# RWKV preparation: head sums and low-rank products from parts, value transposes behind the gram, TensorE in a written order

## The chip, the cores and the metric

One NeuronCore of a Trainium2 chip runs the whole kernel. A core has a matrix engine (TensorE, PE in the profile), a vector engine (VectorE, DVE), an engine for functions of one argument (ScalarE, ACT), a general engine (GpSimd, POOL) and a queue engine for transfers (SyncE, SP). Each works through its own queue of instructions in order; between engines they wait for one another by semaphores. The metric is the device time of one execution in microseconds.

## The reference

One decoder block on 512 tokens of width 1024: RMSNorm, one wide input projection, two mixers (sparse attention and RWKV-7), a gated merge, an output projection, and a gated feed-forward layer. The change concerns the first half of the RWKV mixer, up to the vectors that its recurrence works on:

```python
r, k, v, xw, xa, xg = jnp.split(xl, RWKV_SPLITS, axis=-1)
w = -jax.nn.softplus(-(w0 + jnp.tanh(xw) @ w2)) - 0.5
decay = jnp.exp(-jnp.exp(w.astype(jnp.float32)))
a = jax.nn.sigmoid(a0 + xa @ a2)
...
kk = k * k_k.reshape(H, N).astype(jnp.float32)
kk = kk / jnp.maximum(jnp.sqrt(jnp.sum(kk * kk, axis=-1, keepdims=True)), 1e-12)
k = k * (1.0 + (a - 1.0) * k_a.reshape(H, N).astype(jnp.float32))
...
y = y + jnp.sum(r * k * r_k, axis=-1, keepdims=True) * v
```

There are eight heads of size 64. `xw @ w2` and `xa @ a2` are the two low-rank products (rank 64 each). The two sums over a head's 64 channels, of `kk * kk` and of `r * k * r_k`, are the head sums.

## The kernel before

Dense products are formed from parts: a float32 weight tile `raw` is copied by ScalarE into `whi` (float32r, line 129), VectorE subtracts to get `wlo` (line 339), and a 128-column product takes 24 matmuls of 128x512: 16 with `whi` (against the high and low parts `hh`, `hl` of the normalized input) and 8 with `wlo`. `whi` and `wlo` have two buffers each, so a new tile's parts can be written only when the tile before last has been read. `wnext` loads a tile and splits the next one.

The RWKV preparation works on heads in four pairs, p = 0 to 3, channels on partitions and the 512 tokens along the row. For each pair:

- `front(p)`: dense product for k; the low-rank pair `zw`, `za` from `wa` and `xw` (64 rows each, in the two halves of the array); token shift into `kx` (lines 129, 478); then the decay: `cl` (tanh, scale), a running sum in chunks (`cum`, line 540), and `ep`, `pi` (its exponentials).
- `norms(p)`: squares `kk` on ScalarE, their head sum by a product with a block matrix `ones`, and from it `rn` (maximum on VectorE, line 136; logarithm and exponential on ScalarE).
- `receptance(p)`: dense product for r, shifted into `rx`. `values_of(p)`: dense product for v, into `vx`.
- `values_tok(p)`: four transposes of `vx` on TensorE (line 578), copied into `UV`.
- `vectors(p)`: VectorE's chain from `rx`, `kx`, `rn`, `ep`, `pi` to `AR`, `bh` and `tv`, then the head sum of `tv` (the bonus sum) and `BO`, its product with `vx`.
- `gram(p)`: transposes of `bh` (line 609), copied into `BKT`, and products of `bh` with `AR`, masked into `AB`.

A loop over p runs `front` and `norms` of the next pair, then `values_tok`, `vectors`, `receptance` of the next, `gram`, and `values_of` of the next; one pass of it is called a visit here. Its rows below carry the numbers of the next pair for k, r and v, and those of this pair for the rest. `front(0)`, `norms(0)`, `receptance(0)` and `values_of(0)` stand ahead of the loop.

In this stage no order is written by hand: a scheduler places the instructions of every engine by its own estimates and by which buffers are free, and the outcome is a fixed queue per engine. PSUM has four banks `mm` and two each of `a` and `b`, used in rotation. A visit takes five of the `a` banks in turn (`zw`, squares, bonus sum, transposes, gram), so the gram's first products land in the bank of the bonus sum, which must have been read by `BO`.

Of the kernel before, what the change touches and what calls it, by code (L numbers as in the profile page):

```python
# [12 lines left out]
F32 = mybir.dt.float32  # L13
F32R = mybir.dt.float32r
I32 = mybir.dt.int32
AF = mybir.ActivationFunctionType
ALU = mybir.AluOpType
# [4 lines left out]
S = 512  # L22
D = 1024
NT = S // 128
KT = D // 128
DH = 64
H = 8
NH2 = H // 2
# [55 lines left out]
def hybrid_block(ctx: ExitStack, tc: tile.TileContext, A: dict, out: bass.AP):  # L84
    nc = tc.nc
# [30 lines left out]
    def pa():  # L116
        return bank("a", 2)
# [4 lines left out]
    def mm(o, l, r, start, stop):  # L122
        te.matmul(o, lhsT=l, rhs=r, start=start, stop=stop)  # L123
# [4 lines left out]
    def act(o, i, f=AF.Copy, **kw):  # L128
        sc.activation(o, i, f, **kw)  # L129

    def tt(o, a, b, op):
        return v.tensor_tensor(o, a, b, op=op)  # L132
# [12 lines left out]
    ident, mask, ones, cmask = kc[:, 0:128], kc[:, 128:256], kc[:, 256:384], kc[:, 384:416]  # L145
# [20 lines left out]
    for name in ("rwkv_mu", "rwkv_w0", "rwkv_a0", "rwkv_k_k", "rwkv_k_a", "rwkv_r_k", "rwkv_ln_g", "rwkv_ln_b"):  # L166
        r0, n = ROWS[name]
# [6 lines left out]
    def col(name, i=0):  # L174
        r0, n = ROWS[name]
        return prm[:, r0 + i:r0 + i + 1]
# [41 lines left out]
    hh = hp.tile([128, KT, S], F32R, name="hh", tag="hh")  # L218
# [154 lines left out]
    with tc.manual_schedule(engines={getattr(mybir.EngineType, e) for e in ("PE", "Activation", "DVE", "Pool")}):  # L373
# [10 lines left out]
        for t in range(NT):  # L384
            r = ssx[:, t:t + 1]
# [42 lines left out]
    def run(g):  # L428
        while True:
            try:  # L430
                next(g)
            except StopIteration as e:
                return e.value

    def dense_fm_g(xh, xl, kt=KT):
        hi, lo = wnext(kt, 128)
        p = mmb()
        for k in range(kt):
            mm(p, hi[:, k], xh[:, k], k == 0, False)
            mm(p, hi[:, k], xl[:, k], False, False)  # L440
            if 4 * k == 3 * kt - 4:
                yield
        for k in range(kt):
            mm(p, lo[:, k], xh[:, k], False, k == kt - 1)
        return p

    def dense_fm(xh, xl, kt=KT):
        return run(dense_fm_g(xh, xl, kt))
# [18 lines left out]
    scanm = tp.tile([128, NCH, C], F32, name="scanm")  # L467
    v.memset(scanm, 1.0)
    v.memset(scanm[:, :, 0:1], 0.0)
    wa = tp.tile([128, 512], F32, name="wa")  # L470
    nc.gpsimd.dma_start(wa[0:64], A["rwkv_w2"][0])
    nc.gpsimd.dma_start(wa[64:128], A["rwkv_a2"][0])
    nc.sync.dma_start(g2, A["rwkv_g2"][0])

    def shift_mix(p, m, dst):
        mu = col("rwkv_mu", m)
        act(dst, p, AF.Copy, scale=omm[:, m:m + 1])
        return v.scalar_tensor_tensor(dst[:, 1:], p[:, :-1], mu, dst[:, 1:], op0=ALU.mult, op1=ALU.add)

    def t2(name, bufs=1):  # L480
        return tp.tile([128, S], F32, name=name, tag=name, bufs=bufs)

    xw = t2("xw")
    shift_mix(p0, 12, xw)
    act(xw[0:64], xw[0:64], AF.Tanh)
    shift_mix(dense_fm(hh, hl), 13, sg)

    act(sg, sg, AF.Tanh, scale=0.5)
# [37 lines left out]
    def front(p):  # L526
        cs = slice(128 * p, 128 * p + 128)
        kx = t2("kx", 2)
        pk = dense_fm(hh, hl)
        zw, za = pa(), pb()  # L530
        mm(zw, wa[0:64, cs], xw[0:64], True, True)
        mm(za, wa[64:128, cs], xw[64:128], True, True)
        shift_mix(pk, 4 + p, kx)
        cl = t2("cl")
        act(cl, zw, AF.Tanh, scale=0.5, bias=w0h[:, p:p + 1])
        aa = t2("aa", 2)
        act(aa, za, AF.Tanh, scale=0.5, bias=a0h[:, p:p + 1])
        ts(cl, cl, -0.5 * DECAY, -0.5 * DECAY)
        cum = t2("cum")
        v.tensor_tensor_scan(out=cum, data0=scanm.rearrange("p c t -> p (c t)"), data1=cl, initial=0.0,  # L540
                             op0=ALU.mult, op1=ALU.add)
        ep = tp.tile([128, NCH, C + 1], F32, name="ep", tag="ep", bufs=2)
        v.memset(ep[:, :, 0:1], 1.0)
        act(ep[:, :, 1:], chunks(cum), AF.Exp)
        pi = t2("pi", 2)
        act(pi, cum, AF.Exp, scale=-1.0)
        v.tensor_copy(PC[:, p, :, None], ep[:, :, C:C + 1])
        L[p] = dict(kx=kx, aa=aa, ep=ep, pi=pi)

    def norms(p):  # L550
        kx = L[p]["kx"]
        kk = t2("kk", 2)
        act(kk, kx, AF.Square, scale=col("rwkv_k_k", p))
        ss = pa()
        mm(ss, ones, kk, True, True)
        rn = t2("rn", 2)
        ts(rn, ss, 1e-24, None, op0=ALU.max)
        act(rn, rn, AF.Ln)
        act(rn, rn, AF.Exp, scale=-0.5)
        L[p].update(kk=kk, rn=rn)  # L560

    def receptance(p):
        rx = t2("rx", 2)
        shift_mix(dense_fm(hh, hl), p, rx)
        L[p]["rx"] = rx

    def values_of(p):
        vx = t2("vx")
        mixed = shift_mix(dense_fm(hh, hl), 8 + p, vx)
        if p == NH2 - 1:  # L570
            behind.append(mixed)
        L[p]["vx"] = vx

    def values_tok(p):
        vx = L[p]["vx"]
        pt = pb()
        for i in range(4):
            te.transpose(pt[:, 128 * i:128 * i + 128], vx[:, 128 * i:128 * i + 128], ident)  # L578
        for r in range(2):
            for cc in range(2):  # L580
                act(UV[64 - 64 * r:128 - 64 * r, cc::2, p, r, :],
                    pt[64 * cc:64 * cc + 64].rearrange("p (c r d) -> p c r d", r=2, d=DH)[:, :, r, :])

    def vectors(p):
        kx, aa, ep, pi, kk, rn, rx, vx = (L[p][k] for k in ("kx", "aa", "ep", "pi", "kk", "rn", "rx", "vx"))
        stt(AR[:, p, :, 1, :], chunks(rx), 1.0, ep[:, :, 1:], ALU.mult, ALU.mult)
        stt(kk, kx, col("rwkv_k_k", p), rn, ALU.mult, ALU.mult)
        stt(AR[:, p, :, 0, :], chunks(kk), -1.0, ep[:, :, 0:C], ALU.mult, ALU.mult)
        stt(kk, aa, 1.0, kk, ALU.add, ALU.mult)
        bh = tp.tile([128, NCH, 3, C], F32, name="bh", tag="bh")  # L590
        stt(bh[:, :, 0, :], chunks(kk), 0.5, chunks(pi), ALU.mult, ALU.mult)
        v.tensor_copy(bh[64:128, :, 2, :], bh[64:128, :, 0, :])
        ts(aa, aa, kah[:, p:p + 1], oma[:, p:p + 1])
        stt(kx, kx, 1.0, aa, ALU.mult, ALU.mult)
        stt(bh[:, :, 1, :], chunks(kx), 1.0, chunks(pi), ALU.mult, ALU.mult)
        tv = t2("tv")
        stt(tv, rx, col("rwkv_r_k", p), kx, ALU.mult, ALU.mult)
        L[p]["bh"] = bh
        bs = pa()
        mm(bs, ones, tv, True, True)  # L600
        tt(BO[:, p], bs, vx, ALU.mult)

    def gram(p):
        bh = L[p]["bh"]
# [18 lines left out]


    front(0)
    norms(0)
    receptance(0)
    values_of(0)
    late_params()
    for p in range(NH2):  # L630
        if p + 1 < NH2:
            front(p + 1)
            norms(p + 1)
        values_tok(p)
        vectors(p)
        if p + 1 < NH2:
            receptance(p + 1)
        gram(p)
        if p + 1 < NH2:
            values_of(p + 1)  # L640
        if p + 2 == NH2:
            kcp = dense_fm(hh, hl)
    dbg("AR", AR)
    dbg("BO", BO)
    close(tp_cm)
# [1432 lines left out]
```

## Time and profile before

| what | value |
|---|---|
| median of 3 runs | 797.16 us (796.86 to 798.89) |
| profiled execution, its own time | 796.68 us |
| its span, first to last instruction | 794.9 us |
| granted TensorE clock | 1.000 |
| TensorE busy | 787.9 us (99%) |
| VectorE / ScalarE / GpSimd busy | 640.0 / 468.1 / 121.2 us |
| start of the preparation's pairs to the last gram | 29.7 to 120.4 us |

In the rows that follow, the first number is the start in microseconds from the first instruction, the second the duration; then come engine, line, operation, the tile written and the tiles read, and in brackets the idle time ahead of it with what ended it. Line 123 is the helper for matmuls and line 129 that for ScalarE, so the tiles say which step it is. The profile prints float32r operands of matmuls as f32. A float32 product of 512 columns shows as two rows, or as x2.

### The profile page before, as it was taken

Reading aid. Unit: us, or ns where it says so; the run is one execution under the profiler, and the core shown is the slowest. Engines: PE = TensorE matmul, PEld = TensorE weight load, DVE = VectorE, ACT = ScalarE, POOL = GpSimd, SP = SyncE. Lnnn points to the kernel's source line nnn. Section 1 sums busy time; section 2 is a strip of 40 time slices with the busy share of each in tenths; the row PEclk is TensorE's granted clock in tenths of the full one; section 3 lists DMA queues with packets and bytes.
Section 4 is the critical chain, followed back from the end, with each engine's and each line's share of the span. In section 5 each row is a group of like instructions: output and inputs, shape, how many; then the busy total and the mean of one; then the engine's idle time right before and its main releaser. Section 6 shows DMA issues by size and latency. Waiting matters only on the chain.

```text
span 794.9 us, 15413 instructions
## 1 busy us (share of the span) xinstructions
PE 787.9 (99%) x5901; PEld 674.8 (85%) x5901; DVE 640.0 (81%) x1223; ACT 468.1 (59%) x927; POOL 121.2 (15%) x182
## 2 busy tenths in 40 slices
PE   8999999999999999999999999999999999999998
PEld 7777788887777887788788898999999999987886
DVE  6478869993565588889695589899999999999996
ACT  6765564563454568778444356566666666546552
POOL 6312213023012137332000000000010000101010
PEclk9999999999999999999999999999999999999999
DMA  8996776426679862998148424376798666888741
GB/s 242 294 318 243 267 251 163 121 82 168 185 137 219 190 147 62 176 199 164 55 154 287 129 75 108 110 209 180 233 334 251 186 187 178 288 290 279 269 152 53
DMA packets 155702, 151.78 MB, mean 191 GB/s; under 512 B 7413, under 2 KB 129196, under 8 KB 155628
## 3 DMA queue, kind: packets, MB, share of 16 engines
q1 hardware_dynamic: 139504, 94.90, 41.2%
q0 software_dynamic: 15072, 53.42, 24.7%
q10 hardware_dynamic: 1052, 2.48, 0.9%
q8 instruction: 46, 0.75, 0.4%
q14 instruction: 28, 0.23, 0.1%
HBM read 139.50 MB, written 47.38 MB: 235 GB/s over the span
## 4 chain that ended last, share of the span: by engine, by line
PE 97%; ACT 1%; DVE 1%; DMA 1%; POOL 0%; issue 0%; POOLq 0%; DVEq 0%
PE ps_mm L123 51%; PE ps_mm L126 13%; PE ps_b L126 8%; PE ps_a L126 8%; PE ps_a L123 8%; PE ps_b L123 4%; PE ps_b L1322 1%; PE ps_mm L1322 1%; DMA pra<-in_rwkv_ln_b_dram 1%; POOL pra L171 0%; PE ps_b L609 0%; PE ps_b L578 0%; PE ps_b L209 0%; PE ps_a L939 0%; PE ps_a L1075 0%; PE ps_a L209 0%
## 5 line engine op out<-in xcount | busy, mean ns | idle before, releaser
L129 ACT ACTIVATE whi<-raw 128x1024 fp32r<-128x1024 f32 (+3 forms) x109 | 103.3, 948 | 87.2 <-PE ps_mm L123 55.3
L123 PE MATMUL ps_mm<-hh,whi 128*128 128x512 f32 (+1 forms) x336 | 130.4, 392 | 0.5 <-DVE hl L141 0.5
L123 PE MATMUL ps_mm<-hl,whi 128*128 128x512 f32 (+1 forms) x336 | 128.3, 386 | 0.0
L339 DVE TENSOR_TENSOR wlo<-raw,whi 128x1024 fp32r<-128x1024 f32 (+1 forms) x48 | 54.4, 1133 | 39.2 <-ACT whi L129 22.3
L123 PE MATMUL ps_mm<-hh,wlo 128*128 128x512 f32 (+1 forms) x336 | 80.9, 380 | 0.0
L123 PEld LDWEIGHTS ps_mm<-hh,whi 128*128 128x128 f32 x336 | 63.2, 188 | 16.0 <-issue 1.3
L123 PEld LDWEIGHTS ps_mm<-hl,whi 128*128 128x128 f32 x336 | 63.3, 188 | 11.7 <-issue 1.0
L123 PEld LDWEIGHTS ps_mm<-hh,wlo 128*128 128x128 f32 x336 | 61.1, 188 | 12.3
L234 POOL DMA_DIRECT2D wsum<-in_w_up_dram x48 | 30.1, 654 | 158.9 <-DVE wlo L339 136.0
L132 DVE TENSOR_TENSOR wlo<-raw,whi 128x1024 fp32r<-128x1024 f32 (+1 forms) x48 | 53.1, 1106 | 0.7 <-ACT whi L129 0.7
L129 ACT ACTIVATE whi<-hA 128x1024 fp32r<-128x1024 f32 (+1 forms) x34 | 32.9, 967 | 16.4 <-DVE hA L132 6.5
L129 ACT ACTIVATE P<-P,nm 128x512 f32<-128x512 f32 (+3 forms) x64 | 35.4, 555 | 11.3 <-DVE nm L1248 10.9
L126 PE MATMUL ps_mm<-s,whi 128*128 128x256 f32 x296 | 41.5, 283 | 0.0
L132 DVE TENSOR_TENSOR wlo<-hA,whi 128x1024 fp32r<-128x1024 f32 (+1 forms) x34 | 37.7, 1109 | 4.0 <-ACT whi L129 3.8
L141 DVE SCALAR_TENSOR_TENSOR hA<-ps_mm,cw,hA 128x511 f32<-128x511 f32 (+1 forms) x52 | 38.7, 743 | 1.2 <-ACT hA L129 1.0
L126 PEld LDWEIGHTS ps_mm<-s,whi 128*128 128x128 f32 x296 | 38.2, 192 | 0.0
L1927 POOL DMA_DIRECT2D parked<-s x8 | 4.4, 545 | 209.0 <-DMA raw<-wsum 187.8
L1248 DVE CUSTOM_DVE_ANT_0 P<-ps_a,AB 128x512 f32<-128x512 f32 (+3 forms) x64 | 29.3, 482 | 1.8 <-PE ps_a L123 1.5
L339 POOL TENSOR_TENSOR wlo<-raw,whi 128x512 fp32r<-128x512 f32 (+3 forms) x13 | 21.1, 1626 | 45.3 <-ACT whi L129 19.4
L126 PE MATMUL ps_mm<-s,third 128*128 128x256 f32 x204 | 27.3, 283 | 0.0
L126 PEld LDWEIGHTS ps_mm<-s,third 128*128 128x128 f32 x204 | 25.7, 192 | 0.0
L129 ACT ACTIVATE QK<-ps_mm 128x64 f32<-128x64 f32 (+5 forms) x56 | 14.9, 309 | 17.9 <-PE ps_mm L123 17.8
(519 smaller groups left out, 2124.8 us busy)
## 6 DMA issues: line engine op xcount, KB each, us to landing
wsum<-in_w_up_dram POOLq DMA_DIRECT2D x48, 576.0 KB, 7.3
raw<-in_w_in_dram SPq DMA_DIRECT2D x38, 512.0 KB, 6.8
raw<-wsum SPq DMA_DIRECT2D x43, 256.0 KB, 3.3
wsum<-wsum POOLq DMA_DIRECT2D x16, 576.0 KB, 8.0
raw<-in_w_down_dram SPq DMA_DIRECT2D x17, 512.0 KB, 5.1
raw<-in_w_up_dram SPq DMA_DIRECT2D x31, 256.0 KB, 3.3
hA<-wsum SPq DMA_DIRECT2D x29, 256.0 KB, 4.6
hA<-in_w_down_dram SPq DMA_DIRECT2D x13, 512.0 KB, 3.8
```

Source lines behind the costliest of these rows:

```text
L123: te.matmul(o, lhsT=l, rhs=r, start=start, stop=stop)
L126: te.matmul(o, lhsT=l, rhs=r, start=False, stop=stop, skip_group_check=True)
L129: sc.activation(o, i, f, **kw)
L132: return v.tensor_tensor(o, a, b, op=op)
L141: v.scalar_tensor_tensor(o, a, s, b, op0=op0, op1=op1)
L234: yield nc.gpsimd.dma_start(wsum[j][w], src[w], **({"accum_op": ALU.add} if add else {}))
L339: low = eng.tensor_tensor(lo, raw, hi.bitcast(F32), op=ALU.subtract)
L1248: maxima.append(v.tensor_tensor_reduce(out=P[:, i], in0=o, in1=BT[:, h, 384 - 128 * qt:512], scale=-1.0, scalar=-NEG, op0=ALU.add, op1=ALU ...
L1322: te.transpose(pt[:, 128 * i:128 * i + 128], P[:, 4 * x + i, 128 * k:128 * k + 128], ident)
L1927: move = nc.gpsimd.dma_start(parked[j][:, h], split[j][:, h, 0:4].rearrange("p k n -> p (k n)"))
```

## The change

- `wa` and `xw` become pairs of float32r tiles, a high and a low part. A new scratch tile `ranks` takes the loads and the mixed tokens; ScalarE copies the high parts and VectorE subtracts the low ones. The low-rank pair is formed by three products of parts for each half instead of one float32 product.
- The head sums are formed from parts (`parts`, `head_sums`): ScalarE copies `sumhi`, VectorE subtracts `sumlo`, and two float32r products with `pairs`, a float32r copy of `ones`, replace one float32 product. The first pair's sum of squares stays as it was. `sumhi` and `sumlo` have one buffer each, for both sums.
- `norms` is split: its sum and what follows it (`norms_end`) are called inside `receptance`, between the products with `whi` and those with `wlo`.
- The bonus sum moves from `vectors` to behind `receptance` of the next pair; the value transposes move from behind `front` to the end of the visit, behind `gram`.
- TensorE's queue in the loop is the order of the program's calls; the other engines' queues are still the scheduler's.
- `rx` and `rn` have one buffer instead of two; `cum` is written over `cl`, and `tv` takes the slot of `cl`; `ranks` shares the slot of `bh`, `pairs` that of `prb`.

```diff
-    def dense_fm_g(xh, xl, kt=KT):
+    def dense_fm_g(xh, xl, kt=KT, stop=None):
...
-            if 4 * k == 3 * kt - 4:
+            if k == (3 * kt // 4 - 1 if stop is None else stop):
                 yield
...
-    wa = tp.tile([128, 512], F32, name="wa")
-    nc.gpsimd.dma_start(wa[0:64], A["rwkv_w2"][0])
-    nc.gpsimd.dma_start(wa[64:128], A["rwkv_a2"][0])
+    wa, xw = (tp.tile([128, 2, 512], F32R, name=n) for n in ("wa", "xw"))
+    ranks = tp.tile([128, 2, 512], F32, name="ranks", tag="bh")
+    nc.gpsimd.dma_start(ranks[0:64, 0], A["rwkv_w2"][0])
+    nc.gpsimd.dma_start(ranks[64:128, 0], A["rwkv_a2"][0])
...
-    xw = t2("xw")
-    shift_mix(p0, 12, xw)
-    act(xw[0:64], xw[0:64], AF.Tanh)
+    shift_mix(p0, 12, ranks[:, 1])
+    act(ranks[0:64, 1], ranks[0:64, 1], AF.Tanh)
+    for i, o in ((1, xw), (0, wa)):
+        act(o[:, 0], ranks[:, i])
+        tt(o[:, 1], ranks[:, i], o[:, 0].bitcast(F32), ALU.subtract)
...
-        mm(zw, wa[0:64, cs], xw[0:64], True, True)
-        mm(za, wa[64:128, cs], xw[64:128], True, True)
+        for i, (l, r) in enumerate(((0, 0), (0, 1), (1, 0))):
+            for z, rs in ((zw, slice(0, 64)), (za, slice(64, 128))):
+                mm(z, wa[rs, l, cs], xw[rs, r], i == 0, i == 2)
...
-        cum = t2("cum")
+        cum = cl
...
+    pairs = []
+
+    def parts(x):
+        if not pairs:
+            return ((ones, x),)
+        hi, lo = (tp.tile([128, S], F32R, name=n, tag=n) for n in ("sumhi", "sumlo"))
+        act(hi, x)
+        tt(lo, x, hi.bitcast(F32), ALU.subtract)
+        return (pairs[0], hi), (pairs[0], lo)
+
+    def head_sums(x):
+        o = pa()
+        for i, (l, r) in enumerate(x):
+            mm(o, l, r, i == 0, i == len(x) - 1)
+        return o
+
     def norms(p):
-        kx = L[p]["kx"]
         kk = t2("kk", 2)
-        act(kk, kx, AF.Square, scale=col("rwkv_k_k", p))
-        ss = pa()
-        mm(ss, ones, kk, True, True)
-        rn = t2("rn", 2)
+        act(kk, L[p]["kx"], AF.Square, scale=col("rwkv_k_k", p))
+        L[p].update(kk=kk, squares=parts(kk))
+
+    def norms_end(p):
+        ss = head_sums(L[p]["squares"])
+        rn = t2("rn")
...
-    def receptance(p):
-        rx = t2("rx", 2)
-        shift_mix(dense_fm(hh, hl), p, rx)
+        L[p]["rn"] = rn
+
+    def receptance(p, between=None):
+        rx = t2("rx")
+        product = dense_fm_g(hh, hl, stop=KT - 1)
+        if between:
+            next(product)
+            between()
+        shift_mix(run(product), p, rx)
...
-        tv = t2("tv")
+        tv = tp.tile([128, S], F32, name="tv", tag="cl")
         stt(tv, rx, col("rwkv_r_k", p), kx, ALU.mult, ALU.mult)
-        L[p]["bh"] = bh
-        bs = pa()
-        mm(bs, ones, tv, True, True)
-        tt(BO[:, p], bs, vx, ALU.mult)
+        L[p].update(bh=bh, bonus=tv)
+
+    def bonus(p):
+        tt(BO[:, p], head_sums(L[p]["bonus"]), L[p]["vx"], ALU.mult)
...
-    for p in range(NH2):
-        if p + 1 < NH2:
-            front(p + 1)
-            norms(p + 1)
-        values_tok(p)
-        vectors(p)
-        if p + 1 < NH2:
-            receptance(p + 1)
-        gram(p)
...
+    pairs.append(tp.tile([128, 128], F32R, name="pairs", tag="prb"))
+    act(pairs[0], ones)
+    with tc.manual_schedule(engines={mybir.EngineType.PE}):
+        for p in range(NH2):
+            if p + 1 < NH2:
+                front(p + 1)
+                norms(p + 1)
+            vectors(p)
+            if p + 1 < NH2:
+                receptance(p + 1, functools.partial(norms_end, p + 1))
+            L[p]["bonus"] = parts(L[p]["bonus"])
+            bonus(p)
+            gram(p)
+            values_tok(p)
...
```

How the queues differ is best seen at three places. First ScalarE in the second visit, from the shifted k of the next pair on, before:

```order
L129 ACTIVATE kk<-kx,prm 128x512
L129 ACTIVATE UV<-ps_b 64x4x64
L129 ACTIVATE ep<-cum 128x8x64
L129 ACTIVATE pi<-cum 128x512
L129 ACTIVATE UV<-ps_b 64x4x64 x3
L129 ACT_TABLE_LOAD
L129 ACTIVATE rn<-rn 128x512
L129 ACTIVATE whi<-raw 128x1024
```

and in the changed kernel:

```order
L129 ACTIVATE kk<-kx,prm 128x512
L129 ACTIVATE ep<-cl 128x8x64
L129 ACTIVATE pi<-cl 128x512
L129 ACTIVATE sumhi<-kk 128x512
L129 ACTIVATE whi<-raw 128x1024
L129 ACTIVATE sumhi<-tv 128x512
L129 ACT_TABLE_LOAD
L129 ACTIVATE rn<-rn 128x512
```

The high part of the squares stands behind both exponentials, and the table load for `rn` behind the high part of `tv`. Second, VectorE in the same visit, before:

```order
L540 SCALAR_TENSOR_TENSOR cum<-scanm,cl 128x512
L547 COPY PC<-ep 128x8
L136 TENSOR_SCALAR rn<-ps_a 128x512
L132 TENSOR_TENSOR BO<-ps_a,vx 128x512
L339 TENSOR_TENSOR wlo<-raw,whi 128x1024
L478 SCALAR_TENSOR_TENSOR rx<-ps_mm,prm,rx 128x511
```

and in the changed kernel:

```order
L544 SCALAR_TENSOR_TENSOR cl<-scanm,cl 128x512
L551 COPY PC<-ep 128x8
L141 SCALAR_TENSOR_TENSOR tv<-rx,prm,kx 128x512
L132 TENSOR_TENSOR sumlo<-kk,sumhi 128x512
L136 TENSOR_SCALAR rn<-ps_a 128x512
L132 TENSOR_TENSOR sumlo<-tv,sumhi 128x512
L339 TENSOR_TENSOR wlo<-raw,whi 128x1024
L132 TENSOR_TENSOR BO<-ps_a,vx 128x512
```

`tv` and both low parts stand between the running sum and `wlo`, and `BO` has moved from ahead of `wlo` to behind it. Third, ScalarE at the start of the stage, in the changed kernel, where the row for `wa` is new and the next is the first row that stood there before:

```order
L129 ACTIVATE wa<-ranks 128x512
L129 ACTIVATE whi<-raw 128x1024
L129 ACTIVATE ranks<-ps_mm,omm 128x512
L129 ACT_TABLE_LOAD
L129 ACTIVATE ranks<-ranks 64x512
L129 ACTIVATE whi<-raw 128x1024
L129 ACTIVATE xw<-ranks 128x512
L129 ACTIVATE sg<-ps_mm,omm 128x512
```

The copies of `wa` and `xw` have been put into the queue; the rest keeps its order.

On TensorE, in each of the first three visits, both products of the sum of squares now stand between the sixteen `whi` products and the eight `wlo` products of r, the bonus sum behind the latter, and the value transposes behind the gram.

More of the change, by code (lines that the diff above doesn't have):

```diff
@@ L559, in norms @@
         act(rn, rn, AF.Exp, scale=-0.5)
-        L[p].update(kk=kk, rn=rn)
-    def receptance(p):
-        rx = t2("rx", 2)
-        shift_mix(dense_fm(hh, hl), p, rx)
+        L[p]["rn"] = rn
[6 more added lines that the diff above has]
+        shift_mix(run(product), p, rx)
         L[p]["rx"] = rx
@@ L626, in hybrid_block @@
     norms(0)
+    norms_end(0)
     receptance(0)
@@ L629, in hybrid_block @@
     late_params()
-    for p in range(NH2):
-        if p + 1 < NH2:
-            front(p + 1)
-            norms(p + 1)
-        values_tok(p)
-        vectors(p)
-        if p + 1 < NH2:
-            receptance(p + 1)
-        gram(p)
[L639 to L642, printed above, removed]
+    pairs.append(tp.tile([128, 128], F32R, name="pairs", tag="prb"))
[12 more added lines that the diff above has]
+            values_tok(p)
+            if p + 1 < NH2:
+                values_of(p + 1)
+            if p + 2 == NH2:
+                kcp = dense_fm(hh, hl)
     dbg("AR", AR)
```

## The prediction

> **What bounds the kernel now.** I read the page first: the busy times and the chain of work that ended last.
>
> ```profile
> PE 787.9 (99%) x5901; PEld 674.8 (85%) x5901; DVE 640.0 (81%) x1223; ACT 468.1 (59%) x927; POOL 121.2 (15%) x182
> PE 97%; ACT 1%; DVE 1%; DMA 1%; POOL 0%; issue 0%; POOLq 0%; DVEq 0%
> ```
>
> TensorE is the chain: a microsecond added to or taken from its queue moves the end by as much. Then busy times by stretch, cut at the visits (columns: length, then busy time and instructions of PE, PEld, DVE, ACT, POOL, then granted clock, DMA share, GB/s).
>
> ```profile
> 49.20:71.70 22.50, 22.50 (x133) 17.17 (x132) 17.16 (x27) 14.49 (x21) 3.10 (x7) 1.00 0.71 259
> 71.70:94.20 22.50, 22.50 (x135) 17.18 (x134) 17.18 (x26) 14.49 (x21) 4.41 (x9) 1.00 0.81 280
> ```
>
> A visit takes 22.5 us and TensorE never waits in it. VectorE and ScalarE have 5.3 and 8.0 us to spare, but an in-order TensorE queue asks not whether they have time, but whether one result is there when its product comes up. So the change has two sides: product time saved, and waits on short chains that TensorE did not meet before. TensorE's timeline of the visit at 71.7 (start, duration, instruction):
>
> ```profile
> 71.71 0.69 PE L123 MATMUL ps_a<-xw,wa 64*128 64x512 f32 x1
> 71.72 0.69 PE L123 MATMUL ps_b<-xw,wa 64*128 64x512 f32 x1
> 72.77 0.66 PE L578 MATMUL ps_b<-kc,vx 128*128 128x128 f32 x4
> 73.19 0.48 PE L123 MATMUL ps_mm<-hh,whi 128*128 128x512 f32 x1
> 73.50 0.39 PE L123 MATMUL ps_mm<-hl,whi 128*128 128x512 f32 x1
> 75.34 1.02 PE L123 MATMUL ps_a<-kk,kc 128*128 128x512 f32 x2
> 76.20 1.02 PE L123 MATMUL ps_a<-tv,kc 128*128 128x512 f32 x2
> 76.66 0.79 PE L123 MATMUL ps_mm<-hl,whi 128*128 128x512 f32 x1
> 77.29 0.40 PE L123 MATMUL ps_mm<-hh,whi 128*128 128x512 f32 x1
> 78.68 1.99 PE L123 MATMUL ps_mm<-hh,wlo 128*128 128x512 f32 x8
> 80.60 0.27 PE L609 MATMUL ps_b<-kc,bh 64*128 64x64 f32 x1
> 81.15 0.33 PE L123 MATMUL ps_b<-AR,bh 64*128 64x128 f32 x1
> ```
>
> A product of parts is issued every 0.227 us: eight last 1.99 with a tail of 0.39, so (1.99 - 0.39)/7 = 0.23. Its result can be read when its record ends.
>
> **Product time saved.** The low-rank pair is issued from 71.71 to 72.77, 1.06 us, its two halves side by side; the first product behind full-precision ones takes 0.31 (73.19 to 73.50) instead of 0.23. In parts the pair is three products a half: 3 x 0.23 = 0.69 if the halves still run side by side (they are the same 64-row shapes that do so here), 6 x 0.23 = 1.38 if not. I take the first, since both rows start within 0.01 us: 0.37 saved, and 0.1 of the slow start, 0.5 in all. The two head sums take 75.34 to 77.29 less one product of parts, 1.72; in parts 4 x 0.23 = 0.91: 0.8 saved. So each of three visits is 1.3 shorter, the first front 0.5 (its head sum stays in full precision), and the last visit, with one sum, 0.5.
>
> **The wait for the squares.** In the changed order all sixteen products with whi come first, then both products of the sum of squares. Their parts are made behind the decay: ScalarE copies sumhi after ep and pi; VectorE subtracts sumlo after tv, and tv, now in the slot of cl, must wait until pi has read cl. VectorE and ScalarE in the visit at 71.7:
>
> ```profile
> 69.48 0.75 DVE L141 SCALAR_TENSOR_TENSOR tv<-rx,prm,kx 128x512 f32<-128x512 f32 x1
> 70.15 1.22 DVE L339 TENSOR_TENSOR wlo<-raw,whi 128x1024 fp32r<-128x1024 f32 x1
> 71.94 1.22 DVE L339 TENSOR_TENSOR wlo<-raw,whi 128x1024 fp32r<-128x1024 f32 x1
> 73.08 0.74 DVE L478 SCALAR_TENSOR_TENSOR kx<-ps_mm,prm,kx 128x511 f32<-128x511 f32 x1
> 74.19 1.23 DVE L540 TENSOR_TENSOR_SCAN cum<-scanm,cl 128x512 f32<-128x512 f32 x1
> 76.40 0.69 DVE L136 TENSOR_SCALAR rn<-ps_a 128x512 f32<-128x512 f32 x1
> 77.26 0.69 DVE L132 TENSOR_TENSOR BO<-ps_a,vx 128x512 f32<-128x512 f32 x1 [0.17 <-PE ps_a L123]
> 75.45 0.63 ACT L129 ACTIVATE ep<-cum 128x512 f32<-128x512 f32 x1 [0.29 <-DVE cum L540]
> 75.98 0.61 ACT L129 ACTIVATE pi<-cum 128x512 f32<-128x512 f32 x1
> 79.08 0.63 ACT L129 ACTIVATE rn<-rn 128x512 f32<-128x512 f32 x1
> 79.62 1.04 ACT L129 ACTIVATE whi<-raw 128x1024 fp32r<-128x1024 f32 x1
> ```
>
> wlo, kx, cl and the scan do not move, so pi still ends at 76.59. One ScalarE row follows the next after 0.53 (75.45 to 75.98), so sumhi runs 76.5 to 77.15 (0.63, as rn). tv runs from 76.63, the row behind it starts 0.67 later (69.48 to 70.15): sumlo 77.3 to 77.95. Its cost is not shown; twice its columns take 1.22 and a 512-column one from PSUM 0.69, so 0.6 to 0.69; I take 0.66. [...] TensorE, with the shorter pair, has issued its sixteen by 71.71 + 0.7 + 16 x 0.227 = 76.05: it waits to 77.2 (1.15), issues one, and waits from 77.43 to 78.0 (0.57). Together 1.7 us a visit. If the halves of the pair don't overlap, TensorE arrives 0.7 later but the scan also starts some 0.3 later: 0.35 more a visit in all.
>
> **The wait for BO.** The sum ends at 78.2, the eight wlo products at 80.05, the bonus sum at 80.5 (sumlo of tv is ready at 79.7: rn after the sum's record at 78.4, then the subtraction; no wait), the transposes of bh at 80.5 + 0.6 = 81.1. The gram's first products write the bank of the bonus sum, which BO must have read. VectorE holds the next tile's wlo ahead of BO, and that waits until the eight wlo products have released their buffer, at 80.25: wlo to 81.4, BO to 82.1. TensorE waits 1.0 us. Before, BO ran at 77.26, long before the gram. It costs nothing only if BO goes ahead of wlo.
>
> So a visit: 1.7 + 1.0 - 1.3 = +1.4, three times +4.2. The value transposes cost the same 0.4 at their new place; there they need the BKT copies, two ScalarE rows behind a table load, done 0.4 us before them: free, at most 0.3 if ScalarE runs late. The last visit waits nowhere (two dense products run ahead of its bonus sum) and its sum takes 0.45 instead of the 0.95 between the last two rows of the fence below: -0.5. pairs, the shared rx and rn, and the swapped memset on POOL are covered by whole microseconds.
>
> **The start.** ScalarE now copies wa's high part before the first whi of the pairs, and must have both low-rank loads.
>
> ```profile
> 18.21 0.55 POOL L472 DMA_DIRECT2D wa<-in_rwkv_a_dram  x1
> 22.56 0.55 POOL L505 DMA_DIRECT2D cr<-in_conv_w_dram  x1 [0.40 <-DMA wa<-in_rwkv_a_dram]
> wa<-in_rwkv_a_dram POOLq DMA_DIRECT2D x1, 128.0 KB, 4.1
> 19.13 1.06 ACT L129 ACTIVATE whi<-raw 128x1024 fp32r<-128x1024 f32 x1 [2.69 <-PE ps_mm L123]
> 20.79 1.28 ACT L129 ACT_TABLE_LOAD   x1
> 29.77 0.69 PE L123 MATMUL ps_a<-xw,wa 64*128 64x512 f32 x1
> 29.87 0.69 ACT L129 ACTIVATE kx<-ps_mm,omm 128x512 f32<-128x512 f32 x1 [0.75 <-PE ps_mm L123]
> 32.08 0.72 ACT L129 ACTIVATE kk<-kx,prm 128x512 f32<-128x512 f32 x1
> 32.85 1.13 PE L123 MATMUL ps_a<-kk,kc 128*128 128x512 f32 x2
> 24.23 0.39 PE L123 MATMUL ps_mm<-hh,whi 128*128 128x512 f32 x1
> 117.01 1.02 PE L123 MATMUL ps_a<-tv,kc 128*128 128x512 f32 x2
> 117.96 0.27 PE L609 MATMUL ps_b<-kc,bh 64*128 64x64 f32 x1
> ```
>
> The second load lands at 18.21 + 4.1 = 22.3 to 22.56, so ScalarE's queue restarts at 22.4 instead of 19.13. Through wa 23.0, whi 24.0, xw 24.6, table load 25.8, tanh 26.5, whi 27.5, the high part of xw 28.1, sg 28.7, its tanh behind VectorE's sg 30.1 to 30.7, whi 31.7, kx 32.3, VectorE's wlo and kx 33.6, the squares are there at 34.4 instead of 32.8. TensorE reaches their sum at 29.77 + 0.7 + 8 x 0.227 = 32.3 and waits 2.1, against 0.3 before: +1.8, less the 0.5 saved: +1.3. The first whi (24.0) is just in time for its product at 24.23. A landing at 20.4 would take the 1.8 away; at 22.56 it is 1.9.
>
> **Sum.** +1.3 + 4.2 - 0.5 = +5.0 on the profiled execution's 796.68 (span 794.9 and 1.8 around it) is 801.7. The median shown is 797.16, 0.5 above, so I forecast **802.0**, with 800.5 to 803.5 as its own range. Behind this stage nothing gives it back: TensorE stays the chain there, and the inverse on VectorE, which starts from the last gram, comes 0.4 earlier against TensorE's work than now, since the value transposes then stand behind that gram.
>
> **Rivals.**
> (1) The parts are ready in time and only the savings count: -0.5 - 3.9 - 0.5 = -4.9, **792**. For it: VectorE and ScalarE are idle 5 to 8 us a visit. Against: the rows above put pi's end 0.5 us behind the sixteenth product with two more steps to go. It wins where both parts leave before 76. 8%.
> (2) One wait is missing: without BO's, +5.0 - 3.0 = **799**; without the start's, 800; with half of the squares' wait gone as well as one of these, 797 to 798. For it: sumlo's and the copies' costs are estimates; against: the chain of measured rows alone gives most of it. 15%.
> (3) The pair's halves don't run side by side: +0.35 x 3, and at most as much at the start: **803.3**. 9%.
> (4) The granted clock falls behind the new waits. The rows show 1.00 throughout, but also no wait of 1.7 us within a visit. If the eight products behind each of the four waits ran at half speed, 4 x 1.8 = 7.3 more: **809**. 3%.
> [...]
>
> The forecast itself holds 65%. A measurement of this kernel can tell about 0.3% (2.4 us) from no change. Slower by more: the forecast, (3), (4), less its low tail: 75%. Within: most of (2) and that tail: 15%. Faster: (1) and a little of (2): 10%. The range 797.0 to 804.5 leaves out (1), (4) and the ends.
>
> **What would show it.** In the changed profile: TensorE waiting about 1.1 and 0.6 us for sumhi and sumlo (squares), 1.0 for BO ahead of the AR,bh products, each three times; about 2 us ahead of the first kk product, with ScalarE idle from 16.4 to 22.4; visits of some 23.9 us; the pair issued in 0.7. If the visits are shorter than 22.5, the chain from the scan to sumlo is worked out wrongly; if they are longer but the end is not later, something downstream gave it back.

## The result and the profile after

The changed kernel takes 803.86 us (median of 5 runs, 803.61 to 804.27) against 797.05 us before (796.86 to 798.89, measured beside it): a ratio of 1.0084, 95% interval 1.0073 to 1.0095. It is 6.8 us slower; the forecast was 5.0 slower, on 802.0, with a range of 797.0 to 804.5. The profiled execution went from a span of 794.9 to 802.0, by 7.1. The page of the changed kernel, its busy times and its chain of waits:

```profile
span 802.0 us, 15458 instructions
PE 788.0 (98%) x5909; PEld 676.4 (84%) x5909; DVE 645.3 (80%) x1232; ACT 472.9 (59%) x937; POOL 120.8 (15%) x182
PE 84%; DVE 7%; ACT 3%; issue 3%; DMA 2%; POOL 0%; ACTq 0%; DVEq 0%; POOLq 0%
```

TensorE's busy time is what it was (787.9 before), so all of the 7.1 us shows as idle time of TensorE. This does not mean that nothing was saved: a record counts as busy to its end, also where the next one overlaps it (one from 75.63 to 76.03, the next from 75.86), so issue time that is saved can hide in it. The chain, 97% TensorE before, now leaves it for VectorE and ScalarE. TensorE's list of waits (what it waited for, then us in all, times, longest; the five rows that bear on the change):

```profile
PE ps_a L123 <- ACT sumhi L129: 1.9, 3, 0.6
PE ps_a L123 <- DVE BO L132: 1.6, 3, 0.5
PE ps_a L123 <- ACT kk L129: 1.6, 1, 1.6
PE ps_a L123 <- DVE sumlo L132: 1.1, 3, 0.4
PE ps_mm L123 <- ACT QK L129: 0.9, 1, 0.9
```

The first four are the forecast ones, with the forecast counts; the fifth is new. The idle times count from the end of the record before, 0.39 us long, while products are issued every 0.227, so each wait holds the queue some 0.2 longer than it says here. TensorE's timeline of the visit at 74.4:

```profile
74.39 0.49 PE L123 MATMUL ps_a<-xw,wa 64*128 64x512 f32 x1
74.39 0.49 PE L123 MATMUL ps_b<-xw,wa 64*128 64x512 f32 x1
74.73 0.39 PE L123 MATMUL ps_a<-xw,wa 64*128 64x512 f32 x1
74.96 0.39 PE L123 MATMUL ps_a<-xw,wa 64*128 64x512 f32 x1
75.29 0.50 PE L123 MATMUL ps_mm<-hh,whi 128*128 128x512 f32 x1
75.63 0.40 PE L123 MATMUL ps_mm<-hl,whi 128*128 128x512 f32 x1
79.84 0.50 PE L123 MATMUL ps_a<-sumhi,pairs 128*128 128x512 f32 x1 [0.63 <-ACT sumhi L129]
80.70 0.50 PE L123 MATMUL ps_a<-sumlo,pairs 128*128 128x512 f32 x1 [0.37 <-DVE sumlo L132]
81.04 2.01 PE L123 MATMUL ps_mm<-hh,wlo 128*128 128x512 f32 x8
82.89 0.40 PE L123 MATMUL ps_a<-sumhi,pairs 128*128 128x512 f32 x1
84.98 0.37 PE L123 MATMUL ps_a<-AR,bh 64*128 64x128 f32 x1 [0.54 <-DVE BO L132]
86.96 0.66 PE L603 MATMUL ps_b<-kc,vx 128*128 128x128 f32 x4
```

The halves of the pair do run side by side, and the squares and BO are waited for where the prediction put them. The places by which the span divides are the second and the fourth pair (one half's row each) and q's first product. In the kernel before:

```profile
94.19 0.69 PE L123 MATMUL ps_a<-xw,wa 64*128 64x512 f32 x1
120.44 0.50 PE L123 MATMUL ps_mm<-whi,hh 128*128 128x512 f32 x1
```

and in the changed one:

```profile
50.35 0.49 PE L123 MATMUL ps_a<-xw,wa 64*128 64x512 f32 x1
98.46 0.49 PE L123 MATMUL ps_a<-xw,wa 64*128 64x512 f32 x1
125.88 0.48 PE L123 MATMUL ps_mm<-whi,hh 128*128 128x512 f32 x1
```

With the second pair at 49.25 and the third at 71.71 before, the change by stage is:

| Stage | before | after | change | forecast |
|---|---|---|---|---|
| to the second pair | 49.25 | 50.35 | +1.10 | +1.3 |
| to the third pair | 22.46 | 24.04 | +1.58 | +1.4 |
| to the fourth pair | 22.48 | 24.07 | +1.59 | +1.4 |
| third visit's rest and last visit, to q's first product | 26.25 | 27.42 | +1.17 | +1.4 - 0.5 |
| from there to the end | 674.46 | 676.12 | +1.66 | 0 |
| sum | 794.9 | 802.0 | +7.10 | +5.0 |

The four stages up to q came out at +5.4 where +5.0 was forecast. The other 1.7 is behind q's first product, where the prediction had nothing. There, TensorE's last value transposes and a later product of q, and ScalarE's rows in between:

```profile
125.47 0.66 PE L603 MATMUL ps_b<-kc,vx 128*128 128x128 f32 x4
130.47 0.50 PE L123 MATMUL ps_mm<-whi,hh 128*128 128x512 f32 x1 [0.91 <-ACT QK L129]
126.21 1.06 ACT L129 ACTIVATE spare<-raw 128x1024 fp32r<-128x1024 f32 x1 [1.39 <-issue]
127.30 1.55 ACT L129 ACTIVATE UV<-ps_b 64x256 f32<-64x256 f32 x4
128.87 1.55 ACT L129 ACTIVATE QK<-ps_mm 64x256 f32<-64x256 f32 x4
```

The last pair's value transposes now stand behind the last gram, ScalarE's copies of UV, and then of a PSUM bank that holds another dense product (`kcp` in the kernel, copied to QK), stand behind them, and q's product at 130.47 needs that bank. Before, no such wait is in the list.

At the start ScalarE's first row behind the input and the first head sum read:

```profile
22.22 0.63 ACT L129 ACTIVATE wa<-ranks 128x512 fp32r<-128x512 f32 x1 [5.96 <-issue]
34.20 1.12 PE L123 MATMUL ps_a<-kk,kc 128*128 128x512 f32 x2 [1.56 <-ACT kk L129]
```

ScalarE restarts at 22.22 (forecast 22.4), and the first head sum starts at 34.20 (forecast 34.4, before 32.85).

### The profile page after: what moved, and what is told of

The parts are those of the page before. It is cut to its first block, busy times and chain, and to the rows that moved or that the text cites. A ratio compares the mean times of both kernels' runs of the same rounds, so it can differ in the third digit from the quotient of the medians.

```text
span 802.0 us, 15458 instructions
## 1 busy us (share of the span) xinstructions
PE 788.0 (98%) x5909; PEld 676.4 (84%) x5909; DVE 645.3 (80%) x1232; ACT 472.9 (59%) x937; POOL 120.8 (15%) x182
## 4 chain that ended last, share of the span: by engine, by line
PE 84%; DVE 7%; ACT 3%; issue 3%; DMA 2%; POOL 0%; ACTq 0%; DVEq 0%; POOLq 0%
PE ps_mm L123 44%; PE ps_mm L126 12%; PE ps_a L126 8%; PE ps_b L126 8%; PE ps_a L123 5%; PE ps_b L123 2%; DVE wlo L132 1%; ACT whi L129 1%; DVE wlo L339 1%; PE ps_b L1353 1%; DMA hA<-in_w_down_dram 1%; PE ps_mm L1353 1%; DMA raw<-in_w_down_dram 1%; DVE cl L544 0%; DMA xt<-in_x_dram 0%
```

## The experiments

The theory: the part-wise products do save TensorE's time, and waits on chains that end late eat more than that. The rivals: the part-wise products themselves cost; TensorE's fixed order is at fault; or VectorE and ScalarE set the visit, so that a wait that is taken away turns up further on. Each kernel is the changed one with the edit shown; none leaves work out. Times are medians, with the ratio to the kernel before on the same chip; "visit" is the distance from the second to the third pair of low-rank products, 22.46 before and 24.04 in the change.

| Run | edit | us | ratio to before (95%) | visit |
|---|---|---|---|---|
| e1 | squares' sums later on TensorE | 809.42 | 1.0152 (1.0129 to 1.0176) | 25.90 |
| e2 | bonus's sums behind the gram | 804.95 | 1.0099 (1.0084 to 1.0114) | 24.50 |
| e3 | low-rank loads early | 802.20 | 1.0063 (1.0048 to 1.0078) | 24.03 |
| e4 | last value transposes early | 802.49 | 1.0068 (1.0052 to 1.0085) | 24.08 |
| e5 | squares' parts early | 800.23 | 1.0042 (1.0028 to 1.0056) | 22.93 |
| e6 | gram in another bank | 801.87 | 1.0061 (1.0046 to 1.0077) | 23.50 |
| e7 | e3 + e4 + e5 + e6 | 797.50 | 1.0007 (0.9998 to 1.0016) | 22.91 |
| e8 | head sums whole | 800.46 | 1.0044 (1.0030 to 1.0058) | 23.00 |
| e9 | e7 + value transposes in another bank | 793.60 | 0.9957 (0.9944 to 0.9969) | 21.62 |
| e10 | low-rank pair whole | 802.37 | 1.0070 (1.0056 to 1.0084) | 24.06 |
| e11 | TensorE in the scheduler's order | 803.20 | 1.0076 (1.0060 to 1.0091) | 23.93 |
| e12 | e9 with head sums whole | 796.07 | 0.9989 (0.9980 to 0.9998) | 22.30 |

### e1: the squares' sums later

```diff
-                receptance(p + 1, functools.partial(norms_end, p + 1))
+                receptance(p + 1)
+                norms_end(p + 1)
```

> Edit to the changed kernel: the two products of the squares' head sums stand behind the whole receptance product instead of between its high and low weight passes, so TensorE comes to them about 1.8 us later (the eight hh,wlo passes); nothing else of the change is touched. Theory (the squares' parts come too late for the place given to them): the waits for sumhi and sumlo, 0.63 and 0.37 us before the products in the visits' rows plus about 0.1 us of slow first issue each, go in all three visits; 3 x (1.0 to 1.7) = 3 to 5 us, time 799 to 801. Rival A (the part-wise products themselves cost the time, not their waits): no change, 803.5 to 804.3. Rival B (the wait only moves: the sums of the bonus and the gram stand behind and wait for the same VectorE and ScalarE, whose norm work now starts 1.8 us later): 802 to 804, with a longer wait for BO or for bh in its place.

Measured 809.42, 5.6 slower than the change: all three expectations were too low. The squares' products no longer wait. The bonus's products behind them do; TensorE and VectorE in the visit at 50.35:

```profile
58.27 0.50 PE L123 MATMUL ps_a<-sumhi,pairs 128*128 128x512 f32 x1 [0.83 <-ACT sumhi L129]
60.20 0.49 PE L123 MATMUL ps_a<-sumlo,pairs 128*128 128x512 f32 x1 [1.43 <-DVE sumlo L132]
58.87 0.68 DVE L136 TENSOR_SCALAR rn<-ps_a 128x512 f32<-128x512 f32 x1
59.47 0.68 DVE L132 TENSOR_TENSOR sumlo<-tv,sumhi 128x512 fp32r<-128x512 f32 x1
```

The norm now needs VectorE at 58.87, ahead of the bonus's sumlo: rival B, and worse, because of the clock. The one buffer that both sums share plays a part too: tv is there at 56.0, but ScalarE writes its sumhi only at 57.59, behind rx, and until 57.2 the squares' first product still reads the tile. How much of the two waits the buffer makes by itself, no run here tests. Busy times by stretch of one microsecond (length, then busy time and instructions of PE, PEld, DVE, ACT, POOL, then the granted clock, DMA share, GB/s):

```profile
60.00:61.00 1.00, 0.80 (x9) 0.56 (x11) 1.00 (x3) 0.21 (x1) 0.11 (x1) 0.89 1.02 391
61.00:62.00 1.00, 1.00 (x19) 1.00 (x17) 0.42 (x1) 0.31 (x1) 0.00 (x0) 0.50 1.08 319
112.00:113.00 1.00, 0.68 (x1) 0.29 (x1) 0.87 (x2) 0.33 (x1) 0.62 (x1) 0.50 0.92 274
```

The granted clock was 0.50 from 60.8 to 64.2 in the first visit, from 88.1 to 91.5 in the second, and from 112.0 to 118.8 in the third. (The edges are worked out from the means of such stretches, 0.89 and 0.90, 0.99 and 0.59; in the second visit from the spacing of TensorE's rows and the mean of 0.93 from 76.20 to 102.40.)

From the gram's first transpose to the next dense product it took 4.53, 4.72 and 5.33 us here (60.63 to 65.16, 86.54 to 91.26, 113.05 to 118.38), against 2.89 in e9, which has no wait there (78.08 to 80.97): 1.6, 1.8 and 2.4 more, 5.9 in all. The change, with its wait for BO, takes 3.92 (83.45 to 87.37), so this stretch makes e1 2.8 slower than the change. From the pair to that first transpose it is 1.2, 1.2 and 1.5 slower (10.28, 10.29 and 10.59 against 9.03 and 9.06). Together that is 6.8 of the 6.9 by which the profiled execution (810.58) is slower than that of the change (803.70). At the full clock it would have stood near 804.7 (an estimate, 810.58 - 5.9), close to rival B's band. The four executions agree in direction: 807.01, 808.25, 810.58 and 811.24 at mean granted clocks of 0.998, 0.995, 0.991 and 0.989. A later place is no cover where the same two engines must serve the next product.

### e2: the bonus's sums behind the gram

```diff
-            bonus(p)
             gram(p)
+            bonus(p)
             values_tok(p)
```

> Edit to the changed kernel: the bonus's two sum products stand behind the gram's products, ahead of the value transposes, so that no bank of the gram is free only once VectorE has formed BO. Theory: the three waits for BO (1.6 us in all by the list of TensorE's waits, 0.9 to 1.0 each counted from the queue) go: 803.9 - 3 x 0.9 = 801.2, range 800.5 to 802.5; a share can come back in the last visit, where the value transposes then stand behind two more products. Rival (the gram waits for bh and for its evictions anyway): 803.5 to 804.3.

Measured 804.95, 1.1 slower, which neither had. The wait for BO is gone, and the bonus's sum waits in its place for the bank that ScalarE's copy of BKT reads:

```profile
63.53 0.50 PE L123 MATMUL ps_a<-sumhi,pairs 128*128 128x512 f32 x1 [1.32 <-ACT BKT L129]
```

ScalarE makes that copy behind two table loads and both steps of the norm. The theory had the wait right and its cure wrong.

### e3: the low-rank loads early

```diff
+    with tc.high_priority():
-    nc.gpsimd.dma_start(ranks[0:64, 0], A["rwkv_w2"][0])
-    nc.gpsimd.dma_start(ranks[64:128, 0], A["rwkv_a2"][0])
+        nc.gpsimd.dma_start(ranks[0:64, 0], A["rwkv_w2"][0])
+        nc.gpsimd.dma_start(ranks[64:128, 0], A["rwkv_a2"][0])
```

> Edit to the changed kernel: GpSimd issues both loads of the low-rank weights ahead of its cast at 14.12 us instead of behind it and behind a weight subtraction (15.11 and 18.05 us before). Theory: the second half lands about 18 to 19 us instead of 22.2, ScalarE's copy of it stops holding up the weight copies behind it, ScalarE reaches the first pair's squares about 1 us earlier and the wait of 1.56 us ahead of the first head sum shrinks to a few tenths: 803.9 - 1.1 = 802.8 (the second front's pair of products starts at 49.3 again instead of 50.35). Rival (ScalarE then waits for TensorE's products in the same place, the start is bound by the weight loads): no change, 803.5 to 804.3.

Measured 802.20, 1.7 faster than the change (its four runs, 801.56 to 802.57, lie below all five of the change). GpSimd issues the second load, and ScalarE starts its copy, at:

```profile
14.91 0.54 POOL L474 DMA_DIRECT2D ranks<-in_rwkv_a_dram  x1
20.25 0.63 ACT L129 ACTIVATE wa<-ranks 128x512 fp32r<-128x512 f32 x1 [3.76 <-POOL wlo L339]
```

The second pair starts at 48.92 instead of 50.35: 1.43 of the 1.7. The wait for kk is gone from TensorE's list, so the start's wait is shown, and its cause with it.

### e4: the last value transposes early

```diff
             vectors(p)
+            if p + 1 == NH2:
+                values_tok(p)
...
             gram(p)
-            values_tok(p)
+            if p + 1 < NH2:
+                values_tok(p)
```

> Edit to the changed kernel: the last pair's value transposes stand ahead of its bonus sums and gram, as in the kernel before; the other pairs' stay at the end of the gram. Theory: ScalarE's copies of UV and of the kcp bank start about 4 us earlier, q's first product (ps_mm<-whi,hh) no longer waits 0.91 us for them: 803.9 - 1.2 = 802.7. Rival (the wait for that bank is not what the later 1.2 us come from): 803.5 to 804.3.

Measured 802.49, 1.4 faster (802.10 to 802.73, below all runs of the change). ScalarE's copies, 4.25 and 1.82 earlier than in the change:

```profile
123.05 1.55 ACT L129 ACTIVATE UV<-ps_b 64x256 f32<-64x256 f32 x4 [1.19 <-PE ps_b L603]
127.05 1.54 ACT L129 ACTIVATE QK<-ps_mm 64x256 f32<-64x256 f32 x4
```

From q's first product to the end it is 674.51 us, as before (674.46), and not 676.12, and the wait for QK is gone. So the last stage's loss comes from where the last pair's value transposes stand. Its size is 1.4 by the medians; the 1.66 is one execution's (those of the other kernels that keep these transposes late take 675.4 to 676.0 there).

### e5: the squares' parts early

```diff
-        act(ep[:, :, 1:], chunks(cum), AF.Exp)
+        kk = t2("kk", 2)
+        act(kk, kx, AF.Square, scale=col("rwkv_k_k", p))
+        squares = parts(kk)
+        exp = sc.activation(ep[:, :, 1:], chunks(cum), AF.Exp)
...
+            after(exp, last[0])
+            after(inv, last[0])
+            after(copy, last[1])
```

Here after() puts an instruction behind another of the same engine, last holds the two parts' instructions, inv is the exponential that writes pi and copy is the copy of PC; the bonus's parts, in slots of aa and pi, keep their order ahead of the norm in the same manner.

> Edit to the changed kernel: nothing moves on TensorE; the parts of the squares are formed earlier. ScalarE writes sumhi of kk right behind kk and ahead of the decay exponentials (in the 0.84 us in which it waits for the scan), VectorE writes sumlo right behind the scan and ahead of the copy of PC, and the bonus's parts go to other scratch so that their order stays as it is. Theory: both products of the squares find their operands in place, the waits of 0.63 and 0.37 us and the slow first products go: 3 x 1.7 to 1.9 us, 803.9 - 5.4 = 798.5, range 797.5 to 800.5; the waits for BO stay. Rival (as in the run with the squares late: VectorE and ScalarE set the visit, the wait turns up at the bonus's sums or at BO): 802 to 804.

Measured 800.23, 3.6 faster: the theory's direction, at the slow end of its range. No wait for sumhi or sumlo is left. But the visit shrank by 1.1, not 1.8, and the list has a wait that the change did not show:

```profile
PE ps_b L612 <- ACT BKT L129: 1.1, 3, 0.4
```

(The line is that of the value transposes.) So a part of the rival is true: a wait does turn up further on, though not at the bonus's sums.

### e6: the gram in another bank

```diff
-            ptr = [mmb(), mmb()] if (c0 > 0) == (p < NH2 - 1) else [pb(), pa()]
+            if p < NH2 - 1:
+                ptr = [mmb(), mmb()] if c0 else [pb(), mmb()]
+            else:
+                ptr = [pb(), pa()] if c0 else [mmb(), mmb()]
```

> Edit to the changed kernel: in the first three visits the gram's first half writes one bank of the four that the dense products use in place of the bank that BO is read from; nothing else moves on TensorE. Theory: the three waits for BO (0.55 us of idle in a visit, with the queue and the slow first product about 0.9) go: 803.9 - 2.7 = 801.2, range 800.5 to 802.3. Rival (the gram is held up in the same place by something else, by bh or by its own evictions): 803.5 to 804.3.

Measured 801.87, 2.0 faster than the change, within the range. The wait for BO is gone from the list, and the same new row stands in it: the value transposes wait three times, 0.4 us each, for the copy of BKT.

### e7: the four together

> All four causes taken away together: squares' parts early, low-rank loads early, last values early, gram banks. If the four waits are all that eats the savings, their sum comes off: 803.9 - 5.4 - 2.7 - 1.7 - 1.4 = 792.7, range 791.5 to 795, which is faster than the kernel before (797.05) and near the 792 that the prediction gave for the savings alone. Rival (the waits hide each other or VectorE sets the visit): 797 to 801.

Measured 797.50: 6.4 faster than the change, where the gains of the four alone add up to 8.7 (3.63 + 1.99 + 1.66 + 1.37). In the visits TensorE has one wait left; its row and ScalarE's row of the copy:

```profile
60.64 0.66 PE L613 MATMUL ps_b<-kc,vx 128*128 128x128 f32 x4 [1.23 <-ACT BKT L129]
60.01 0.58 ACT L129 ACTIVATE BKT<-ps_b 128x512 f32<-128x512 f32 x1
```

The value transposes at their new place write the bank that the gram's transposes of bh wrote, and ScalarE must first have copied it to BKT. In the changed kernel the copy ended at 86.33 and the transposes came at 86.96: free, but only because the waits ahead of them had made TensorE late.

### e8: the head sums whole

```diff
-        if not pairs:
+        if True:
             return ((ones, x),)
```

> Edit to the changed kernel: the head sums are single float32 products again in every visit (0.86 us each instead of two of 0.23), with no parts formed on ScalarE and VectorE; the low-rank pair, the place of the sums, of the value transposes and TensorE's fixed order stay as in the change. Theory: the squares' wait goes (kk ends at 53.2, TensorE comes at 55.2), the saving of about 0.4 us a product goes too: 803.9 - 3 x 1.8 + 6 x 0.4 to 7 x 0.4 = 800.9 to 801.3, range 799.5 to 802.5. Rival A (the part-wise sums are a gain even with their waits): 804.5 to 806.5. Rival B (TensorE's fixed order is what costs, whatever the sums): 803.5 to 806.

Measured 800.46, 3.4 faster than the change, near the theory's 801. With the waits that they bring, the part-wise sums are a loss.

### e9: all five waits away

```diff
-        pt = pb()
+        pt = pa() if p < NH2 - 1 else pb()
```

(on top of e7, in values_tok)

> The four together as before, and one edit more: in the first three visits the value transposes write a bank of the other pair of single-purpose banks (the one BO is read from) instead of the one that ScalarE's copy of BKT still reads. In the run of the four the first value transpose started at 60.64 us, 1.23 us of idle after the gram's last product; with the queue, about 1.5 us behind the place that it could have had (59.1). Theory: this fifth wait, which the other waits had covered, is what kept the four from adding up: 797.5 - 3 x 1.5 = 793.0, range 792.0 to 794.5, faster than the kernel before. Rival (VectorE sets the visit by now: from its wlo at 49.38 to the one at 72.29 it idles only some 4.5 us): 795 to 797.5, with waits at bh or BO in place of it.

Measured 793.60 (793.45 to 793.81), 10.3 faster than the change and 0.43% faster than the kernel before. The list of TensorE's waits has no row of the visits any more. Its timeline at 70.43:

```profile
70.43 0.49 PE L123 MATMUL ps_a<-xw,wa 64*128 64x512 f32 x1
71.32 0.50 PE L123 MATMUL ps_mm<-hh,whi 128*128 128x512 f32 x1
75.08 0.40 PE L123 MATMUL ps_a<-sumhi,pairs 128*128 128x512 f32 x1
75.32 0.40 PE L123 MATMUL ps_a<-sumlo,pairs 128*128 128x512 f32 x1
75.55 1.98 PE L123 MATMUL ps_mm<-hh,wlo 128*128 128x512 f32 x8
80.56 0.66 PE L613 MATMUL ps_a<-kc,vx 128*128 128x128 f32 x4
```

VectorE does not set the visit at 21.62 us: the rival of e7 and e9 falls. This visit also measures the waits of the change: its gain over 24.04 is 2.42 us. By distance from the visit's first pair, the passes with wlo start 5.12 us in here (75.55) and 6.65 in the change (81.04): 1.53 for the squares, and the value transposes 10.13 and 12.57: 0.91 more, for BO and what stands around it.

### e10: the low-rank pair whole

```diff
-        for i, (l, r) in enumerate(((0, 0), (0, 1), (1, 0))):
-            for z, rs in ((zw, slice(0, 64)), (za, slice(64, 128))):
-                mm(z, wa[rs, l, cs], xw[rs, r], i == 0, i == 2)
+        mm(zw, wa[0:64, cs], xw[0:64], True, True)
+        mm(za, wa[64:128, cs], xw[64:128], True, True)
```

(with wa and xw one float32 tile each, as before the change)

> Edit to the changed kernel: the low-rank pair is one float32 product each again (two halves side by side), its weights loaded straight, no parts formed; the head sums and all the rest stay as in the change. Theory: the start's wait goes (1.1 to 1.7 us less), each of the four fronts pays 0.3 to 0.5 us more for the pair: 803.9 - 1.4 + 4 x 0.4 = 804.1, range 803.2 to 805. Rival A (the pair's parts are a plain gain, the start's wait comes from elsewhere): 805 to 806. Rival B (the part-wise pair saves nothing, halves not side by side): 802 to 803.

Measured 802.37 (801.93 to 803.89), 1.5 faster than the change, in the band of rival B, but not for its reason: the halves do run side by side in the change. The second pair comes at 49.30 (1.05 earlier), and the visits are as long as in the change. Two rows say why:

```profile
73.36 0.69 PE L123 MATMUL ps_a<-xw,wa 64*128 64x512 f32 x1
74.42 0.50 PE L123 MATMUL ps_mm<-hh,whi 128*128 128x512 f32 x1
```

The whole pair takes 1.06 us up to the next product. The pair in parts takes 0.90 (74.39 to 75.29 in the change): its three products hold the queue for 0.34, 0.23 and 0.33, not three times 0.23, and the product behind it is as slow (0.34) as behind the whole pair. It saves 0.16, not 0.5, and in the change even that only lengthens the wait for the squares (0.63 against 0.45 here). So in this kernel the pair's parts are a loss by the start that they delay. (The 0.16 is read from these rows; no run has the whole pair without the other waits.)

### e11: TensorE in the scheduler's order

```diff
-    with tc.manual_schedule(engines={mybir.EngineType.PE}):
+    if True:
```

> Edit to the changed kernel: TensorE's fixed order is dropped for the four visits, and the scheduler places its instructions: the squares' first product goes behind five of the eight low-weight passes, the second behind all of them, the bonus's products into the gram, and the gram's transposes and products go half by half (all that write one bank, then all that write the other) instead of in turn. Theory: the waits for sumhi, sumlo and BO shrink by 2 us or so a visit; but halves that no longer run side by side cost: sixteen transposes at 0.06 and sixteen products at 0.11 us a pair would take twice as long, 0.5 + 0.9 us a visit, in all four visits: 803.9 - 3 x 2 + 4 x 1.4 = 803.5, range 800 to 806. Rival (the fixed order is at fault and its waits are the whole loss): under 799.5. Rival (the sums' waits turn up behind it as with the squares late): 806 to 810.

Measured 803.20, as the change but for 0.7. Busy times from 50 to 100:

```profile
50.00:100.00 50.00, 49.98 (x281) 38.97 (x280) 39.24 (x58) 32.56 (x49) 8.19 (x17) 1.00 0.81 280
```

TensorE hardly waits, and yet the visit is 23.93. Its transposes and products of 64 rows now go largely one bank after the other instead of two side by side: with the bonus's two products among them and the value transposes, the gram takes from 81.63 to 87.42, 5.8 us, where e9 needs 3.6 for the same work (77.37 to 80.97). The order is not at fault; without it the time goes to another cause.

### e12: the head sums whole, without waits

e9 with the edit of e8.

> The kernel with all five waits taken away, with one thing undone: the head sums are single float32 products (0.86 us each) again, no parts are formed for them; the pair, the banks, the loads and the places stay. With no wait left on TensorE in the visits this is the price of the sums' parts by itself. Theory: each of the seven sums that come after the first costs 0.3 to 0.4 us more, 793.6 + 7 x 0.35 = 796.0, range 795.3 to 796.8, and the visits last 22.3 us instead of 21.62. Rival A (the parts save nothing even when they are in time, or ScalarE and VectorE pay for them): 793.0 to 794.2. Rival B (without the parts VectorE and ScalarE run earlier and another cover opens): under 793.

Measured 796.07, which is 2.5 slower than e9, as the theory had it (796.0). TensorE's rows:

```profile
76.29 1.02 PE L123 MATMUL ps_a<-kk,kc 128*128 128x512 f32 x2
76.74 2.42 PE L123 MATMUL ps_mm<-hh,wlo 128*128 128x512 f32 x8
```

The visit is 22.30 and not 21.62, so two sums in parts save 0.68, and that is most of the saving that the change had to offer in a visit.

## Why the prediction was right or wrong

**Direction and range: right, and by the mechanism forecast.** TensorE was the chain, and the short chains decide, not the spare time of VectorE and ScalarE. The size is off: +5.0 forecast, +6.8 by the medians and +7.1 by the profile.

**The step that failed** is "The last visit waits nowhere", with "free, at most 0.3" for the value transposes at their new place. In the last visit they cost 1.4 us, behind the visit, where the prediction had nothing (e4; 1.66 in the profiled execution): what stands behind them on ScalarE, UV and the copies of the kcp bank, is what q waits for, and the prediction costed the transposes by what they need, not by who needs them. In the other visits they were free as forecast, but under the cover of the other waits; with that cover gone they cost 1.3 us a visit (e7 against e9, 22.91 to 21.62). The prediction named the copies of BKT as their condition and did not say what would happen without the cover.

**The start:** +1.10 against +1.3, by the mechanism forecast. The early loads took 1.7 away (e3), the whole pair 1.05 at the same place (e10).

**The squares and BO:** 1.53 and 0.91 a visit, forecast 1.7 and 1.0. ScalarE's sumhi, VectorE's sumlo behind tv, and BO behind wlo are all as worked out, within 0.2 us of the forecast distances from the visit's pair. VectorE's sumlo of the squares:

```profile
79.96 0.68 DVE L132 TENSOR_TENSOR sumlo<-kk,sumhi 128x512 fp32r<-128x512 f32 x1
```

The prediction took 0.66 for it, an estimate from two rows of before (1.22 and 0.69); the row shows 0.68.

**The savings** were the other mis-sized term: 0.84 a visit (22.46 before, 21.62 in e9) where 1.3 was taken. The sums give 0.68 (e12), forecast 0.8; the pair 0.16, forecast 0.5, as the three products of a half were costed at the rate inside a long run of 128-row products. This error (0.46) and that of the waits (0.26, in the other direction) cancel in part, and so it is partly luck that the visit came out at +1.58, near its +1.4.

**The rivals.** (1), the savings alone at 792, is near what e9 shows (793.6), for which all five waits must go. (2) and (3) did not come: all waits are there and the halves run side by side. (4), the clock behind new waits, did not come in the change (1.00 throughout), but it did in e1 (0.50), at waits of 0.83 and 1.43 that are each shorter than the 1.7 and 2.1 at which the prediction gave it 3%, its author's estimate.

**"Nothing gives it back"** held: from q's first product to the end the kernel with e4's edit takes what it took before.

## What to carry to other kernels

Where an in-order TensorE is the chain, the price of a faster product is whether its operands are in place when it comes up: split a product in parts only where the parts' last step ends ahead of it, and move that step, not the product (e5, which also gives the second sum's parts scratch of their own, against e1). Cost a moved instruction by what it frees for whom (its bank, the copies queued behind it) and not by its own needs alone. A wait can cover the next one, so take all away together before the savings are judged: here four edits gave 6.4 us, and a fifth, which was worth nothing in the changed kernel by its list of waits, 3.9 more.

## What the runs showed of the hardware

The granted clock fell to 0.50 in all three visits of e1, at idle stretches of 0.83 and 1.43 us (1.44 in the second) with one product between them, and stayed there for 3.4, 3.4 and 6.8 us (60.8 to 64.2, 88.1 to 91.5, 112.0 to 118.8). The second of the two stretches ended at 60.20, 86.11 and 112.32: the first two falls came 0.6 and 2.0 us behind its end, the third 0.3 ahead of it. Waits of 0.63 and 0.37 (the change) left the clock at 1.00, and so did single ones of 1.23 (e7), 1.32 (e2) and 1.56 (the first head sum of the change). What sets the clock, and why 1.56 in another place went without a fall, no run here shows.

In the change, the product behind those of 64 rows at 75.29 and the one behind the wait at 80.70 hold the queue for 0.34 us instead of 0.23 (75.29 to 75.63, 80.70 to 81.04), and the 64-row pair behind the wait for BO holds it for 0.21 instead of 0.11 (84.98 to 85.19, then 85.30). At the three waits of a visit this is a tenth of a microsecond each that the list of waits does not show.
